# The modulation product of a conditioned encoder layer: from split float32r matmuls to plain float32 on four column groups

## The chip, the cores and the metric

The kernel runs on one core of one Trainium2 chip. The metric is the device time of one execution in microseconds, as a median over runs. Engines are named as the profile names them: PE is TensorE's matmul side, PEld its weight loads, DVE is VectorE, ACT is ScalarE, POOL is GpSimd, SP is SyncE, whose queue issues the loads and stores.

## The reference, cut to what matters

One step of an encoder layer: 512 prompt tokens and 8 sequences of 16 tokens each. Every one of the 9 sequences (1 prompt, 8 samples) has a conditioning vector c of 1024 numbers. Six vectors of 1024 numbers are made of it, two each of shift, scale and gate:

```
m = jax.nn.silu(c) @ w_ada + b_ada            # (9, 1024) @ (1024, 6144)
shift1, scale1, gate1, shift2, scale2, gate2 = split(m, 6)
h = rmsnorm(x) * (1 + scale1) + shift1         # input of the projections and of both attentions
x = x + gate1 * (merge(attentions) @ w_out)
h = rmsnorm(x) * (1 + scale2) + shift2
x = x + gate2 * ((silu(h @ w_gate) * (h @ w_up)) @ w_down)
```

All is float32. The product with w_ada, 24 MB of weights for nine rows, is what the change touches.

## The kernel before, in words

Most products are made of float32r matmuls (one pass over the moving columns). To keep float32's accuracy, each operand is split into a high part (a cast to float32r on ScalarE, L85) and a low part (source minus high, L86, on VectorE or, where `eng=G` is given, on GpSimd), and the products high x high, high x low and low x high are added in PSUM (L92 to L94).

Weights come in granules of 512 KB, 128 partitions by 1024 numbers. `load_raw` (L168) loads one into the pool `w_raw`, which has three buffers for all weights of the kernel; `granule` splits it into `w_hi` and `w_lo`, three buffers each per pool.

`ada_chunk` makes 512 of the 6144 columns of m. Twelve chunks make all. A chunk is four granules of w_ada, each two blocks of 128 rows. The stationary operand is `cT`: per block of 128 rows, 9 columns of the high part of silu(c) and 9 of the low part. For each of the 8 blocks one matmul has the granule's high part as its moving operand (L198) and one its low part (L199), so 16 matmuls of 512 columns add up in 18 rows of one PSUM bank. Row r and row 9 + r belong to sequence r.

These 18 rows are brought together later. `ada_cols` (L211) multiplies blocks of 128 columns of the rows, with the row of b_ada as a nineteenth, by the selector `sel` (19 by 9), and so adds high, low and bias and turns rows into columns. `gate_rows` does the same for the gates with `selr`, which also spreads a sequence's row over its tokens.

Order of the work: the stage of the modulation and the input norm follows a list written out by hand (`steps`): n are key norms of the cached keys of a sequence, x loads and norms of 128 tokens, c loads the selectors, a0 to a3 are the chunks 0 to 3 (shift1 and scale1), h and s modulate. In it three of four granules of a chunk are subtracted on GpSimd (`engs=(None, G, G, G)`), and the chunk's rows stay in SBUF. Chunks 4 to 10 come between the gate blocks that fill the attention of the prompt, chunk 11 at the end of the attention of the sample; their rows go to `ada_d` in DRAM and are loaded again by `ada_rows`. A planner that simulates the engines sets the order in which each engine's instructions stand, so that matmuls of a chunk can stand apart, with others between them.

Other lines that are named: L289 to L298 norm and transpose x, L319 and L320 are squares and sums of the key norms, `lTh` and `lTl` are high and low parts of transposed cached latents, L102 to L109 the reciprocal square root, L395 to L397 products of the rotary tables, L834 and L924 plain float32 matmuls of the attention of the sample: L834 (`absorb`) in batches of four, on partitions 0 to 63 and 64 to 127 in turn, L924 (`mla_values`) five for each of two blocks and eight sequences.

Of the kernel before, what the change touches and what calls it, by code (L numbers as in the profile page):

```python
# [42 lines left out]
QSC = QK ** -0.5  # L43
C_KV, C_QB, C_KB, C_VB, C_G = 384, 672, 1184, 1696, 2208
# [3 lines left out]
def layer_kernel(  # L48
# [47 lines left out]
    def rsqrt(out, ss, inv, pl, n):  # L96
        v = pl.tile([P, n], F32, tag="rs_v", bufs=2, name=nm("rsv"))
        t = pl.tile([P, n], F32, tag="rs_t", bufs=2, name=nm("rst"))
        if not isinstance(inv, list):
            inv = [(0, n, inv)]  # L100
        for a, b, sc in inv:
            V.tensor_scalar(out=v[:, a:b], in0=ss[:, a:b], scalar1=sc, scalar2=EPS, op0=ALU.mult, op1=ALU.add)  # L102
        # a square root of the scalar engine's table, then a Newton step to float32
        for a, b, sc in inv:
            S.activation(out=t[:, a:b], in_=ss[:, a:b], func=AF.Sqrt, scale=sc, bias=eps_t)
        V.reciprocal(out, t)
        V.tensor_tensor(out=t, in0=out, in1=out, op=ALU.mult)  # L107
        V.scalar_tensor_tensor(out=t, in0=t, scalar=-0.5, in1=v, op0=ALU.mult, op1=ALU.mult)
        V.scalar_tensor_tensor(out=out, in0=t, scalar=1.5, in1=out, op0=ALU.add, op1=ALU.mult)  # L109
# [10 lines left out]
    # ---------------------------------------------------------------- constants  # L120
# [10 lines left out]
    # the tensor engine's clock rises while the first loads are under way  # L131
# [8 lines left out]
    sel = ct([19, 9], "sel")  # L140
    selr = ct([19, 2 * P], "selr", F32R)
# [7 lines left out]
    cT = ct([P, KD, 18], "cT", F32R)  # L149

    ada_d = dram.tile([18, 6 * DM], F32, tag="ada_d", name="ada_d")
# [9 lines left out]
    # weight staging: 0.5 MB granules, each split exactly into a high and a low part  # L161
    wa = ctx.enter_context(pool("wstA", side="right"))

    def load_raw(src, shape, rows=P):
        n = shape[0] * shape[1]
        raw = wa.tile([P, 1024], F32, tag="w_raw", bufs=3, name=nm("wraw"))[:rows, :n]
        rv = raw.rearrange("p (k n) -> p k n", k=shape[0])
        nc.sync.dma_start(rv, src)  # L168
        return raw, rv
# [21 lines left out]
    def ada_chunk(pls, rowp, ci, keep=None, engs=(None,)):  # L191
        ps = mm_tile()
        for g in range(4):
            hi, lo = granule(pls[g % len(pls)], w_ada_v[:, 2 * g:2 * g + 2, ci * 512:(ci + 1) * 512], [2, 512],
                             eng=engs[g % len(engs)])
            for j in range(2):
                k = 2 * g + j
                T.matmul(ps[:18, :], cT[:, k, :], hi[:, j, :], start=(k == 0), stop=False)  # L198
                T.matmul(ps[:18, :], cT[:, k, :], lo[:, j, :], start=False, stop=(k == 7))  # L199
        if keep is not None:  # L200
            S.copy(keep, ps[:18, :])
        else:
            row = rowp.tile([18, 512], F32, tag="ada_row", bufs=2, name=nm("adar"))
            S.copy(row, ps[:18, :])
            nc.sync.dma_start(ada_d[:, ci * 512:(ci + 1) * 512], row)
# [14 lines left out]
    # ---------------------------------------------------------------- state of the sample up to its attention  # L220
# [33 lines left out]
    # ---------------------------------------------------------------- modulation, normed input, norms of cached keys  # L254
    with pool("klat") as kp, pool("xin") as xp:
        xnT = xp.tile([P, KD, NT], F32, tag="xnT", name="xnT")
        c_sb = xp.tile([19, DM], F32, tag="rows", bufs=1, name="c_sb")[0:9, :]
# [25 lines left out]
        split(cT[:, :, 0:9], cT[:, :, 9:18], ptv)  # L283
# [41 lines left out]
        def ada_start(ci):  # L325
            if ci % 2 == 0:
                rows[0] = xp.tile([19, DM], F32, tag="rows", bufs=1, name=nm("rows1"))
                nc.sync.dma_start(rows[0][18:19, :], b_ada[:, ci * 512:ci * 512 + DM])
            ada_chunk(AB, None, ci, keep=rows[0][0:18, (ci % 2) * 512:(ci % 2 + 1) * 512], engs=(None, G, G, G))
            if ci == 1:  # L330
                ada_shift(B1, ada_cols(rows[0], 8))
            if ci == 3:
                ada_scale(A1, ada_cols(rows[0], 8), gmix)

        # h^T = xn^T * A + B, split
# [17 lines left out]
        def consts(_):  # L353
            nc.sync.dma_start(sel, sel_tab[:, 2 * P:])
            nc.sync.dma_start(gmix, g_norm_mix[0].rearrange("(k p) -> p k", p=P))
            nc.sync.dma_start(gffn, g_norm_ffn[0].rearrange("(k p) -> p k", p=P))
            V.tensor_copy(selr, load_raw(sel_tab[:, 0:2 * P].unsqueeze(1), [1, 2 * P], 19)[0])
# [5 lines left out]
    # small constants of the attention part  # L363
# [38 lines left out]
    def split3(dst, src, order):  # L402
        # parts of src, 32 columns each, side by side: high and low parts in the order given
        first = order.index("h")
        hi = dst[:, :, first * 32:(first + 1) * 32]
        S.copy(hi, src)
        for i, o in enumerate(order):
            d = dst[:, :, i * 32:(i + 1) * 32]
            if o == "h" and i != first:
                S.copy(d, src)  # L410
            elif o == "l":
                V.tensor_tensor(out=d, in0=src, in1=f(hi), op=ALU.subtract)

    # ---------------------------------------------------------------- projections out of the modulated input
# [216 lines left out]
    # relative-bias table, its clipped far end extended, distance rising along the row  # L631
# [20 lines left out]
    # ---------------------------------------------------------------- attention of the prompt, beside the gates  # L652
# [5 lines left out]
    def gate_block(blk, pl):  # L658
        # sigmoid(z) = (1 + tanh(z / 2)) / 2; the sum and the factor come with the merge
        hi, lo = granule(wa, w_in_v[:, :, C_G + blk * P:C_G + (blk + 1) * P], [KD, P])  # L660
        sg = pl.tile([P, NT], F32, tag="gsg", bufs=2, name=nm("sg"))
        for hf in range(2):
            ps = mm_tile()
            c = slice(hf * HALF, (hf + 1) * HALF)
            for k in range(KD):
                mm3(ps[:, :HALF], hi[:, k, :], lo[:, k, :], hT[:, k, c], hTl[:, k, c], k == 0, k == KD - 1)
                if k % 4 == 3:
                    yield
            S.activation(out=sg[:, c], in_=ps[:, :HALF], func=AF.Tanh, scale=0.5)
        nc.sync.dma_start(gate_d[blk], sg)  # L670
# [3 lines left out]
    def filler(blocks, pl):  # L674
        for n in blocks:
            yield from gate_block(n, pl)
            if n in ADA_AT:
                ada_chunk((wa,), pl, 4 + ADA_AT.index(n))
                yield
# [5 lines left out]
    with pool("pwork") as pw:  # L685
# [17 lines left out]
        def head_in(n):  # L703
            br, h = n // H, n % H
            st = {"br": br, "h": h, "bias": None}
            if h % 2 == 0:
                vn = load_nat(vb_d if br else va_d, P, h // 2 * P, "vnat")
                # stationary of a head: its high and low parts side by side, the high part at the head's rows
                st["v"] = pt_([P, 4, 4, 64], "v", 2, F32R)
                split(st["v"][:, :, 0::3, :], st["v"][:, :, 1:3, :], vn.rearrange("p j (h d) -> p j h d", h=2), eng=G)  # L710
            else:
                st["v"] = heads[n - 1]["v"]
# [86 lines left out]
    # ---------------------------------------------------------------- attention of the sample  # L799
    e2 = {}  # L800
    with pool("ework") as ew:
# [23 lines left out]
        def absorb():  # L825
            # q' = Wk (g qn) per head
# [139 lines left out]
        def band_probs(st):  # L966
            # per pair of heads: stationary [high | low] parts of its 32 rows of probabilities
# [45 lines left out]
        # operations of a step: lower case on the sequence before, upper case on this one  # L1013
# [4 lines left out]
        for s in range(NSEQ + 1):  # L1018
            for op in "N K0 S0 v0 K1 v1 S1 K2 S2 v2 K3 S3 X p v3 K u o Y P A".split():
# [7 lines left out]
                elif s < NSEQ:  # L1027
# [18 lines left out]
                    elif s == NSEQ - 1:  # L1046
                        ada_chunk((wa,), ew, 11)
# [15 lines left out]
    # ---------------------------------------------------------------- merge of the branches  # L1063
# [12 lines left out]
    def ada_rows(c0):  # L1076
        raw = wa.tile([P, 1024], F32, tag="w_raw", bufs=3, name=nm("wraw"))
        nc.sync.dma_start(raw[0:18, :], ada_d[:, c0:c0 + DM])
        nc.sync.dma_start(raw[18:19, :], b_ada[:, c0:c0 + DM])
        return raw[0:19, :]  # L1080

    def gate_rows(c0, scale):
        # rows of a gate, by tokens: of the prompt, of the sample
        raw = ada_rows(c0)
        hi = wa.tile([P, 1024], F32R, tag="w_hi", bufs=3, name=nm("whi"))[0:19, :]
        lo = wa.tile([P, 1024], F32R, tag="w_lo", bufs=3, name=nm("wlo"))[0:19, :]
# [56 lines left out]
    # ---------------------------------------------------------------- output projection, residual, second norm  # L1143
# [79 lines left out]
    # ---------------------------------------------------------------- feed-forward  # L1223
# [61 lines left out]
def _tables():  # L1285
    """Rotary tables of the positions, and selectors of the modulation rows: of the shapes alone."""
# [40 lines left out]
```

## Time and profile before

| | us |
|---|---|
| median of 3 runs | 1216.45 |
| lowest, highest | 1215.79, 1216.54 |
| profiled execution, first to last instruction | 1215.7 |
| TensorE matmuls busy | 1189.0 (98%) |
| VectorE busy | 684.2 (56%) |
| ScalarE busy | 544.3 (45%) |
| GpSimd busy | 137.9 (11%) |

Times in the profile are microseconds from the span's start, durations of single instructions nanoseconds where marked mean ns. A matmul's duration overlaps that of the next; how fast they follow each other is read from start to start. A plain float32 matmul is recorded as two instructions. Shapes stand as partitions x elements; for matmuls rows*columns of the stationary operand, then the moving one.

### The profile page before, as it was taken

Reading aid. Unit: us, or ns where it says so; the run is one execution under the profiler, and the core shown is the slowest. Engines: PE = TensorE matmul, PEld = TensorE weight load, DVE = VectorE, ACT = ScalarE, POOL = GpSimd, SP = SyncE. Lnnn points to the kernel's source line nnn. Section 1 sums busy time; section 2 is a strip of 40 time slices with the busy share of each in tenths; the row PEclk is TensorE's granted clock in tenths of the full one; section 3 lists DMA queues with packets and bytes.
Section 4 is the critical chain, followed back from the end, with each engine's and each line's share of the span. In section 5 each row is a group of like instructions: output and inputs, shape, how many; then the busy total and the mean of one; then the engine's idle time right before and its main releaser. Section 6 shows DMA issues by size and latency. Waiting matters only on the chain. (4 is left out here: it accounts for less than half of the span.)

```text
span 1215.7 us, 19702 instructions
## 1 busy us (share of the span) xinstructions
PE 1189.0 (98%) x7515; PEld 1077.5 (89%) x7515; DVE 684.2 (56%) x1539; ACT 544.3 (45%) x1086; POOL 137.9 (11%) x253
## 2 busy tenths in 40 slices
PE   8889999999999999999999998999999999999998
PEld 6568988999987889899989888999989999889996
DVE  4887566858887775777766437433344233342333
ACT  6775533446776665666653246322112222112210
POOL 2440001010000101334212221000000000000000
PEclk9998999999999999999999998999999999999999
DMA  8651434475655348455367312322123222232111
GB/s 260 227 161 46 127 137 136 159 235 167 184 162 176 119 137 287 138 178 173 95 213 266 103 55 70 88 70 78 62 70 105 70 71 87 67 89 70 70 40 65
DMA packets 159264, 155.30 MB, mean 128 GB/s; under 512 B 24632, under 2 KB 123475, under 8 KB 159170
## 3 DMA queue, kind: packets, MB, share of 16 engines
q1 hardware_dynamic: 159170, 154.05, 40.4%
q8 instruction: 59, 0.97, 0.3%
q14 instruction: 35, 0.29, 0.1%
HBM read 135.15 MB, written 18.88 MB: 127 GB/s over the span
## 5 line engine op out<-in xcount | busy, mean ns | idle before, releaser
L85 ACT CAST whi<-wraw 128x1024 fp32r<-128x1024 f32 (+2 forms) x184 | 190.3, 1038 | 273.4 <-PE mm L94 107.5
L86 DVE TENSOR_TENSOR wlo<-wraw,whi 128x1024 fp32r<-128x1024 f32 (+3 forms) x168 | 203.4, 1213 | 131.6 <-ACT whi L85 127.3
L92 PE MATMUL mm<-h2T,whi 128*128 128x320 f32 x704 | 217.9, 311 | 0.0
L93 PE MATMUL mm<-h2Tl,whi 128*128 128x320 f32 x704 | 217.8, 310 | 0.0
L94 PE MATMUL mm<-h2T,wlo 128*128 128x320 f32 x704 | 217.8, 310 | 0.0
L92 PEld LDWEIGHTS mm<-h2T,whi 128*128 128x128 f32 x704 | 132.9, 189 | 0.4 <-ACT aT L85 0.4
L93 PEld LDWEIGHTS mm<-h2Tl,whi 128*128 128x128 f32 x704 | 132.7, 189 | 0.1
L94 PEld LDWEIGHTS mm<-h2T,wlo 128*128 128x128 f32 x704 | 132.7, 189 | 0.0
L1237 DVE TENSOR_TENSOR sg<-mm,sg 128x320 f32<-128x320 f32 x44 | 21.6, 492 | 121.3 <-PE mm L94 119.3
L93 PE MATMUL mm<-wlo,aT 128*128 128x512 f32 x220 | 85.5, 389 | 0.0
L92 PE MATMUL mm<-whi,aT 128*128 128x512 f32 x220 | 85.5, 389 | 0.0
L94 PE MATMUL mm<-whi,aTl 128*128 128x512 f32 x220 | 85.4, 389 | 0.0
L92 PE MATMUL mm<-hT_hi,whi 128*128 128x320 f32 x256 | 81.5, 318 | 0.0
L94 PE MATMUL mm<-whi,hT_lo 128*128 128x512 f32 (+3 forms) x240 | 79.6, 332 | 0.0
L94 PE MATMUL mm<-hT_hi,wlo 128*128 128x320 f32 x256 | 79.5, 311 | 0.0
L93 PE MATMUL mm<-hT_lo,whi 128*128 128x320 f32 x256 | 79.4, 310 | 0.0
L92 PE MATMUL mm<-whi,hT_hi 128*128 128x512 f32 (+3 forms) x240 | 79.4, 331 | 0.0
L93 PE MATMUL mm<-wlo,hT_hi 128*128 128x512 f32 (+3 forms) x240 | 79.4, 331 | 0.0
L1268 DVE TENSOR_TENSOR tmp<-mm,gate 128x512 f32<-128x512 f32 x30 | 20.7, 690 | 78.7 <-PE mm L94 78.7
L85 ACT CAST aT<-sg 128x320 fp32r<-128x320 f32 x44 | 20.0, 455 | 78.7 <-DVE sg L1237 78.7
L92 PEld LDWEIGHTS mm<-hT_hi,whi 128*128 128x128 f32 x256 | 48.2, 188 | 2.1 <-issue 1.2
L94 PEld LDWEIGHTS mm<-hT_hi,wlo 128*128 128x128 f32 x256 | 48.1, 188 | 1.2 <-DVE wlo L86 0.3
(343 smaller groups left out, 2672.4 us busy)
## 6 DMA issues: line engine op xcount, KB each, us to landing
wraw<-in_w_ada_dram SPq DMA_DIRECT2D x48, 512.0 KB
wraw<-in_w_in_dram SPq DMA_DIRECT2D x28, 512.0 KB
wraw<-in_w_gate_dram SPq DMA_DIRECT2D x22, 512.0 KB
wraw<-in_w_up_dram SPq DMA_DIRECT2D x22, 512.0 KB
wraw<-in_w_down_dram SPq DMA_DIRECT2D x22, 512.0 KB
lat<-in_cache_kv_latent_dram SPq DMA_DIRECT2D x16, 512.0 KB
wraw<-in_cache_band_v_dram SPq DMA_DIRECT2D x16, 512.0 KB
kn<-in_cache_band_k_dram SPq DMA_DIRECT2D x16, 512.0 KB
```

The lines of the kernel that those rows point to most:

```text
L85: S.copy(hi, src)
L86: (eng or V).tensor_tensor(out=lo, in0=src, in1=f(hi), op=ALU.subtract)
L92: T.matmul(out, lh, rh, start=start, stop=False)
L93: T.matmul(out, lh, rl, start=False, stop=False)
L94: T.matmul(out, ll, rh, start=False, stop=stop)
L1237: V.tensor_tensor(out=sg, in0=pu[:, :HALF], in1=sg, op=ALU.mult)
L1268: V.tensor_tensor(out=tmp, in0=ps, in1=gate2[t // 4][:, cc], op=ALU.mult)
```

## The change

The product is made in plain float32, so nothing of w_ada and of silu(c) is split any more. A matmul has 32 columns of the stationary operand (9 of silu(c), the rest zeros) and writes one of four groups of 32 PSUM partitions: block k of the 8 goes to group k mod 4, and a group adds up two blocks. The four groups of a chunk are added later by the same selectors, which now have 106 rows (9 in each group of 32, and the bias).

```
+AR = 3 * 32 + 9 + 1
...
-    sel = ct([19, 9], "sel")
-    selr = ct([19, 2 * P], "selr", F32R)
+    sel = ct([AR, 9], "sel")
+    selr = ct([AR, 2 * P], "selr", F32R)
+    G.memset(sel, 0.0)
...
-    cT = ct([P, KD, 18], "cT", F32R)
-    ada_d = dram.tile([18, 6 * DM], F32, tag="ada_d", name="ada_d")
+    cT = ct([P, KD, 32], "cT")
+    V.memset(cT, 0.0)
+    ada_d = dram.tile([AR - 1, 6 * DM], F32, tag="ada_d", name="ada_d")
...
-    def load_raw(src, shape, rows=P):
+    def load_raw(src, shape, rows=P, given=P):
...
-        nc.sync.dma_start(rv, src)
+        if given < rows:
+            G.memset(raw, 0.0)
+        nc.sync.dma_start(rv[:given], src)
...
-    def ada_chunk(pls, rowp, ci, keep=None, engs=(None,)):
+    def ada_chunk(rowp, ci, keep=None):
         ps = mm_tile()
         for g in range(4):
-            hi, lo = granule(pls[g % len(pls)], w_ada_v[:, 2 * g:2 * g + 2, ci * 512:(ci + 1) * 512], [2, 512],
-                             eng=engs[g % len(engs)])
+            rv = load_raw(w_ada_v[:, 2 * g:2 * g + 2, ci * 512:(ci + 1) * 512], [2, 512])[1]
             for j in range(2):
                 k = 2 * g + j
-                T.matmul(ps[:18, :], cT[:, k, :], hi[:, j, :], start=(k == 0), stop=False)
-                T.matmul(ps[:18, :], cT[:, k, :], lo[:, j, :], start=False, stop=(k == 7))
+                q = slice(32 * (k % 4), 32 * (k % 4) + 32)
+                T.matmul(ps[q, :], cT[:, k, :], rv[:, j, :], start=(k < 4), stop=(k >= 4))
         if keep is not None:
-            S.copy(keep, ps[:18, :])
+            S.copy(keep, ps[:AR - 1, :])
         else:
-            row = rowp.tile([18, 512], F32, tag="ada_row", bufs=2, name=nm("adar"))
-            S.copy(row, ps[:18, :])
+            row = rowp.tile([AR - 1, 512], F32, tag="ada_row", bufs=2, name=nm("adar"))
+            S.copy(row, ps[:AR - 1, :])
             nc.sync.dma_start(ada_d[:, ci * 512:(ci + 1) * 512], row)
...
-        split(cT[:, :, 0:9], cT[:, :, 9:18], ptv)
+        S.copy(cT[:, :, 0:9], ptv)
...
         def consts(_):
-            nc.sync.dma_start(sel, sel_tab[:, 2 * P:])
+            raw = load_raw(sel_tab[0:9, 0:2 * P].unsqueeze(1), [1, 2 * P], AR, 9)[0]
+            nc.sync.dma_start(sel[AR - 1:AR, :], sel_tab[18:19, 2 * P:])
+            nc.sync.dma_start(raw[AR - 1:AR, :], sel_tab[18:19, 0:2 * P])
+            for q in range(4):
+                nc.sync.dma_start(sel[32 * q:32 * q + 9, :], sel_tab[0:9, 2 * P:])
+                if q:
+                    nc.sync.dma_start(raw[32 * q:32 * q + 9, :], sel_tab[0:9, 0:2 * P])
...
-            V.tensor_copy(selr, load_raw(sel_tab[:, 0:2 * P].unsqueeze(1), [1, 2 * P], 19)[0])
+            V.tensor_copy(selr, raw)
```

Everywhere else 18 rows become 105 and 19 become 106: the tiles `rows`, the rows that `ada_rows` loads, and their split in `gate_rows`.

## Rows read from the trace of the kernel before

**Rows 1.** Page: busy us (share of the span) and instructions of each engine.

```profile
PE 1189.0 (98%) x7515; PEld 1077.5 (89%) x7515; DVE 684.2 (56%) x1539; ACT 544.3 (45%) x1086; POOL 137.9 (11%) x253
```

**Rows 2.** Windows: stretch, length, busy (count) of PE PEld DVE ACT POOL, clock, DMA.

```profile
25.00:45.00 20.00, 15.90 (x71) 10.05 (x70) 17.66 (x40) 13.45 (x24) 8.07 (x4) 0.91 0.74 252
...
270.00:465.00 195.00, 195.00 (x1230) 166.00 (x1229) 157.02 (x426) 135.04 (x303) 8.68 (x12) 1.00 0.53 161
465.00:620.00 155.00, 149.47 (x1360) 142.18 (x1358) 105.52 (x265) 97.62 (x221) 48.19 (x178) 1.00 0.53 169
```

**Rows 3.** Groups by line, TensorE, by shape: count, busy us, mean ns, idle before.

```profile
L198 PE MATMUL mm<-whi,cT 128*18 128x512 f32 x96 | 39.7, 413 | 0.0
...
L924 PE MATMUL mm<-PT,lat 128*128 128x128 f32 x128 | 18.1, 275 | 0.0
...
L211 PE MATMUL tr<-sel,rows 19*128 19x9 f32 x32 | 4.2, 255 | 1.1 <-ACT rows L201 1.1
```

**Rows 4.** Timeline of TensorE inside chunk 9: start us, us, instruction.

```profile
426.11 0.39 PE L198 MATMUL mm<-whi,cT 128*18 128x512 f32 x1
...
427.27 0.40 PE L199 MATMUL mm<-wlo,cT 128*18 128x512 f32 x1
```

**Rows 5.** Timeline of TensorE, 488 to 493 us, neighbours of one kind merged.

```profile
488.13 0.31 PE L94 MATMUL mm<-hT_hi,wlo 128*128 128x320 f32 x1
488.38 2.26 PE L834 MATMUL mm<-qnT,wkT 64*128 64x128 f32 x24
...
491.59 1.16 PE L834 MATMUL mm<-qnT,wkT 64*128 64x128 f32 x8
```

**Rows 6.** Line L834: duration ns least/median/most, first and last start.

```profile
L834 PE MATMUL mm<-qnT,wkT x32: 272/272/373, 488.4 to 492.5; 64*128 64x128 f32 x32
```

**Rows 7.** Groups by line and shape, ScalarE, VectorE, GpSimd (GpSimd before 90 us).

```profile
L85 ACT CAST whi<-wraw 128x1024 fp32r<-128x1024 f32 x174 | 182.3, 1051 | 268.8 <-PE mm L94 107.5 <-PE mm L93 99.4 <-DMA wraw<-in_w_up_dram 16.0
...
L86 DVE TENSOR_TENSOR wlo<-wraw,whi 128x1024 fp32r<-128x1024 f32 x158 | 192.9, 1223 | 128.7 <-ACT whi L85 124.3 <-DMA kn<-in_cache_band_k_dram 1.4 <-PE mm L94 1.1
...
L86 POOL TENSOR_TENSOR wlo<-wraw,whi 128x1024 fp32r<-128x1024 f32 x12 | 29.1, 2432 | 42.0 <-ACT whi L85 26.6 <-DVE rn_all L109 9.5 <-PE mm L199 5.8
```

**Rows 8.** Timeline of VectorE.

```profile
29.74 0.23 DVE L396 TENSOR_TENSOR rq_s<-rq_s,gqr_bc 128x80 f32<-128x80 f32 x1
29.89 2.38 DVE L397 TENSOR_TENSOR rq_s<-rq_s,gqr_bc 128x80 f32<-128x80 f32 x1
...
47.23 2.07 DVE L107 TENSOR_TENSOR rst<-rn_all 128x32 f32<-128x32 f32 x1
```

**Rows 9.** Timeline of GpSimd.

```profile
29.77 2.40 POOL L86 TENSOR_TENSOR wlo<-wraw,whi 128x1024 fp32r<-128x1024 f32 x1 [0.74 <-ACT whi L85]
41.73 7.53 POOL L86 TENSOR_TENSOR wlo<-wraw,whi 128x1024 fp32r<-128x1024 f32 x3 [9.55 <-DVE rn_all L109]
```

**Rows 10.** Timeline of TensorE in the first stage; in brackets idle time and releaser.

```profile
28.14 0.40 PE L93 MATMUL mm<-wk_lo,lTh 128*128 128x512 f32 x1
29.87 0.50 PE L94 MATMUL mm<-wk_hi,lTl 128*128 128x512 f32 x1 [1.33 <-DVE lTl L86]
...
30.45 0.40 PE L93 MATMUL mm<-wk_lo,lTh 128*128 128x512 f32 x1
33.61 0.79 PE L94 MATMUL mm<-wk_hi,lTl 128*128 128x512 f32 x1 [2.77 <-DVE lTl L86]
...
49.26 0.40 PE L198 MATMUL mm<-whi,cT 128*18 128x512 f32 x1
50.41 0.96 PE L94 MATMUL mm<-wk_hi,lTl 128*128 128x512 f32 x3 [0.75 <-DVE rsv L102]
```

**Rows 11.** Window, TensorE alone: stretch, length, busy (count), granted clock, DMA, GB/s.

```profile
33.70:37.00 3.30, 3.30 (x8) 0.50 0.99 350
```

**Rows 12.** Timeline of SP's queue: start us, us of issuing.

```profile
6.31 0.29 SPq L354 DMA_DIRECT2D sel<-in_sel_tab_dram  x1
...
11.25 0.37 SPq L168 DMA_DIRECT2D wraw<-in_w_ada_dram  x1
```

More of the change, by code (lines that the diff above doesn't have):

```diff
@@ L256, in layer_kernel @@
         xnT = xp.tile([P, KD, NT], F32, tag="xnT", name="xnT")
-        c_sb = xp.tile([19, DM], F32, tag="rows", bufs=1, name="c_sb")[0:9, :]
+        c_sb = xp.tile([AR, DM], F32, tag="rows", bufs=1, name="c_sb")[0:9, :]
         nc.sync.dma_start(c_sb[0:1, :], c_prompt)
@@ L326, in ada_start @@
             if ci % 2 == 0:
-                rows[0] = xp.tile([19, DM], F32, tag="rows", bufs=1, name=nm("rows1"))
-                nc.sync.dma_start(rows[0][18:19, :], b_ada[:, ci * 512:ci * 512 + DM])
-            ada_chunk(AB, None, ci, keep=rows[0][0:18, (ci % 2) * 512:(ci % 2 + 1) * 512], engs=(None, G, G, G))
+                rows[0] = xp.tile([AR, DM], F32, tag="rows", bufs=1, name=nm("rows1"))
+                nc.sync.dma_start(rows[0][AR - 1:AR, :], b_ada[:, ci * 512:ci * 512 + DM])
+            ada_chunk(None, ci, keep=rows[0][0:AR - 1, (ci % 2) * 512:(ci % 2 + 1) * 512])
             if ci == 1:
@@ L677, in filler @@
             if n in ADA_AT:
-                ada_chunk((wa,), pl, 4 + ADA_AT.index(n))
+                ada_chunk(pl, 4 + ADA_AT.index(n))
                 yield
@@ L1046, in layer_kernel @@
                     elif s == NSEQ - 1:
-                        ada_chunk((wa,), ew, 11)
+                        ada_chunk(ew, 11)
             mla, band = mla_n, nxt
@@ L1077, in ada_rows @@
         raw = wa.tile([P, 1024], F32, tag="w_raw", bufs=3, name=nm("wraw"))
-        nc.sync.dma_start(raw[0:18, :], ada_d[:, c0:c0 + DM])
-        nc.sync.dma_start(raw[18:19, :], b_ada[:, c0:c0 + DM])
-        return raw[0:19, :]
+        nc.sync.dma_start(raw[0:AR - 1, :], ada_d[:, c0:c0 + DM])
+        nc.sync.dma_start(raw[AR - 1:AR, :], b_ada[:, c0:c0 + DM])
+        return raw[0:AR, :]
     def gate_rows(c0, scale):
         raw = ada_rows(c0)
-        hi = wa.tile([P, 1024], F32R, tag="w_hi", bufs=3, name=nm("whi"))[0:19, :]
-        lo = wa.tile([P, 1024], F32R, tag="w_lo", bufs=3, name=nm("wlo"))[0:19, :]
+        hi = wa.tile([P, 1024], F32R, tag="w_hi", bufs=3, name=nm("whi"))[0:AR, :]
+        lo = wa.tile([P, 1024], F32R, tag="w_lo", bufs=3, name=nm("wlo"))[0:AR, :]
         split(hi, lo, raw)
```

## The prediction, made before the changed kernel was run

> **What bounds the kernel now.** I read the page first: TensorE is busy for 98% of the span [rows 1]. An average can hide a stage with another limit, so next come the windows by stage. From 270 to 465 us TensorE has no gap at all, from 25 to 45 us it is busy for 15.9 us of 20, and from 465 to 620 us for 149.5 of 155 [rows 2]. The reader is to see two regimes. In the middle, only TensorE's own instructions count, and time freed on ScalarE or VectorE is worth nothing. In the first 62 us TensorE also waits, so there the splitting work can matter. The four chunks 0 to 3 of the modulation product lie in the first 80 us; chunks 4 to 10 lie in the attention of the prompt and chunk 11 at 605 us, where TensorE is the bound.
>
> Third come the groups by line. L198 and its twin L199 run 96 times each [rows 3]. Their mean of 413 ns overlaps the next instruction; what counts is the distance from start to start, read in the timeline: six starts from 426.11 to 427.27 us, (427.27 - 426.11) / 5 = 0.232 us [rows 4]. A chunk of 16 thus costs 16 x 0.232 = 3.71 us, and a granule (a load of two blocks of 128 rows, four matmuls) 0.93 us.
>
> **What is removed.** 192 matmuls at 0.232 us = 44.5 us of TensorE; 48 casts on ScalarE at 1.05 us; 36 subtractions on VectorE at 1.22 us and 12 on GpSimd at 2.43 us [rows 7].
>
> **What is added on TensorE: 96 plain float32 matmuls of 32 columns by 512.** The trace has no such matmul, but it has plain float32 ones of another shape. Each is recorded as two instructions: L924 is called 64 times with lat (8 sequences, 2 blocks, 4 keys) and shows x128 [rows 3]. So 96 calls become 192 instructions, as many as before, and the question is what one costs and how many run at once.
>
> Cost of one, called U. The last eight of L834 (128 columns) take 1.16 us for x8 [rows 5]; less the last one's 0.272 and the 0.373 - 0.272 = 0.10 by which the first waits for its weights [rows 6], 0.79 / 7 = 0.112 us from start to start. Four times as many columns give at most 4 x 0.112 = 0.448 us. L211, with only 9 columns, lasts nearly as long (255 against 275 ns [rows 3]), so part of 0.112 may be the weight load, and 0.448 is an upper bound. From below, a plain pass is not quicker than the 0.232 of the same columns in one pass. I take 0.448, since L834 and L924 are of the same kind and L198 is not. The Trainium skill (FP8 and Floating Point Precision, TensorE Precision Notes) says that true float32 takes four passes through the array; as an estimate that is 4 x 512 / 2.4 GHz = 0.853 us a matmul, 0.427 an instruction, and the sum below would end some 2 us lower; no row here separates the passes.
>
> How many at once. Every matmul of before starts at the first column, so no row shows column groups side by side. The nearest are the row groups of L834: three batches of eight, on rows 0 to 63 and 64 to 127 in turn. One after another, 24 would have 0.10 + 23 x 0.112 = 2.68 us from first start to last; measured is 2.26 - 0.27 = 1.99 [rows 5]. The 0.69 saved are six instructions at two borders, three at each: one batch's tail runs beside the next one's head, and more than the two neighbours overlap. I take it that column groups behave likewise: four streams at once. This is the step with most doubt.
>
> Length of a run. Raw granules live in a pool of three. Before, the split freed a slot; now a slot is held until TensorE has read it, so at most three of a chunk's four granules are at hand together. In the middle I reckon with a run of six matmuls and one of two per chunk (8 chunks), in the first stage with runs of two, as the granules come one by one (16 runs). Each run costs 0.1 us to enter: L834 starts 0.25 us after the L94 ahead of it, whose 320 columns need 0.13 at 2.4 GHz [rows 5]; bounds 0 and 0.2. With four streams, a run of two takes 2 U + 0.1 = 1.00 us against 0.93, and a run of six, in which two groups serve twice, 4 U + 0.1 = 1.89. First stage: 16 x 0.07 = **+1.1 us**. Middle: 8 x (1.89 + 1.00 - 3.71) = **-6.6 us**.
>
> **What the splits gave back.** While GpSimd subtracts (29.77 us, for 2.40) VectorE's L397 takes 2.38 us, where its neighbour L396, of the same kind, takes 0.23; at 47.23 a small L107 takes 2.07 under three GpSimd subtractions that begin at 41.73 [rows 8, 9]. TensorE waits behind these: 29.87 - 28.14 - 0.23 = 1.50 us, 33.61 - 30.45 - 0.23 = 2.93 us (both for lTl), 50.41 - 49.26 - 0.23 = 0.92 us [rows 10]. After the second wait the granted clock is 0.50 (1.2 GHz) for 3.3 us [rows 11], which costs half of that, 1.7 us. With no GpSimd subtraction there, all four can go: 1.50 + 2.93 + 0.92 + 1.7 = **-7.0 us**; at worst nothing, if TensorE is then late for the next load instead. ScalarE's and VectorE's other savings are costed at nothing: behind 195.0 busy us of 195 nobody waits for them [rows 2]; without that cover the 36 VectorE subtractions alone would be worth 44 us.
>
> **What is moved or grows.** The selectors now come in ten loads in place of two, all in SP's queue ahead of the first w_ada granule. From the load of sel to that granule's issue SP takes 11.25 - 6.31 = 4.9 us for five issues; one plain issue is 0.29 [rows 12]. Eight more are 2.4 to 3 us by which x, cached keys and w_ada come later; TensorE has work of loads already made, so I take **+1.0 us**, bounds 0 and 3. Behind the cast of selr, which waits for those loads, stand VectorE's norms; the same bound covers it. The memset of cT and sel, and results of 105 rows in place of 18 (copies by columns, a write of 215 KB per chunk), are costed at nothing: their cover is the same full TensorE; without it they are a microsecond in all.
>
> Sum: +1.1 - 6.6 - 7.0 + 1.0 = -11.5 us, from a span of 1215.7 to 1204.2. The median of the runs, 1216.45, is 0.75 above the span, so the forecast is **1205 us**.
>
> **The rivals.** *Two streams only.* If a record may not start before the one ahead of it has, then a group's second record waits for its first, and the next group stands behind both: just the second of one and the first of the next run together, and n matmuls take n + 1 units. A run of two costs 3 U + 0.1 = 1.44 us, a run of six 7 U + 0.1 = 3.24. That is 16 x 0.51 = +8.2 and 8 x (3.24 + 1.44 - 3.71) = +7.8; with -7.0 and +1.0, +10 us: 1226. For it: the two records of a matmul stand side by side. Against it: three overlaps at a border of L834, where this allows one. The Trainium skill (TensorE: Matmul & The Clock Gate, Part 3, The mechanism) states this order, matmuls starting and ending strictly in program order. The trace agrees only in part, since the 1.99 us of L834 need more than one overlap per border, unless the batches were interleaved in the queue.
>
> *No streams at once (the change does not do what its groups are for).* All instructions run singly: a run of two 4 U + 0.1 = 1.89, a chunk 16 U + 0.2 = 7.37. 16 x 0.96 + 8 x 3.66 = +44.7, with -6.0 +38.7: 1255 us. This is the case on the slower side; it decides as soon as U exceeds 0.23 by more than the 6 us pay for, at U = 0.25. For it: no row shows two column groups, and each would need its own stream of all 128 rows. Against it: L834's two groups do run together.
>
> *Cheap passes.* With U = 0.232 and four streams a chunk's runs cost 6 x 0.232 + 0.2 = 1.59 us and the sum is some -30 us, 1187. Against it: two records of 128 columns never start less than 0.11 apart within a group.
>
> **How the numbers follow.** Four streams 0.47, with its own range 1192 to 1217 (units of 0.40, whole chunks in one run, against no stall recovered, 3 us of queue and entries of 0.2); two streams 0.22; none 0.28; cheap passes 0.03. The range 1192 to 1254 leaves out the cheap passes, the fastest tenth of the first case and the upper half of the third. About 0.2%, 2.4 us, is what a measurement of this kernel can tell from no change. Faster: 0.44 of the first case and the last, 0.47. Same: the upper end of the first and the lower of the second, 0.07. Slower: 0.46.
>
> **What would show it.** In the changed profile: 192 records of 512 columns with 32 active columns; four of them starting within some ns of one another and the next four 0.45 us later (four streams), or pairs (two), or single starts 0.45 apart (none). No GpSimd work on w_ada, no VectorE instruction of 128x32 over 1 us before 62 us, TensorE's waits for lTl near 30 us gone and the granted clock there at 1.0. The prediction is wrong if column groups do not overlap, if TensorE waits on w_ada loads because slots are freed late, or if the first stage's stalls only move.

## The result, and the profile after

The changed kernel takes 1246.82 us (median of 4 runs, 1244.86 to 1248.15) where the kernel before took 1216.12 beside it (4 runs, 1214.93 to 1216.54): a ratio of 1.0255, 95% interval 1.0241 to 1.027. It is 30.7 us slower; the forecast was 1205. The profiled execution has a span of 1244.8 us.

First the page of the changed kernel (busy us, share, instructions) against [rows 1]:

```profile
PE 1197.8 (96%) x7515; PEld 1075.8 (86%) x7515; DVE 637.4 (51%) x1503; ACT 502.4 (40%) x1038; POOL 102.5 (8%) x243
```

TensorE has as many instructions as before, but its share fell from 98% to 96%: it waits more, while every other engine has less to do. The windows, with the columns of [rows 2], say where:

```profile
25.00:45.00 20.00, 15.28 (x76) 8.69 (x76) 11.24 (x40) 9.58 (x22) 0.00 (x0) 0.91 0.72 233
45.00:62.00 17.00, 17.00 (x89) 10.37 (x85) 9.62 (x24) 8.72 (x18) 0.00 (x0) 1.00 0.76 248
...
270.00:465.00 195.00, 181.06 (x1109) 150.32 (x1108) 122.47 (x369) 101.61 (x251) 8.59 (x12) 0.95 0.51 150
465.00:620.00 155.00, 147.08 (x1278) 137.84 (x1277) 98.74 (x252) 91.03 (x205) 43.80 (x176) 0.98 0.54 169
```

From 45 to 62 us TensorE has no gap. But from 270 to 465 us, where TensorE had 195.00 busy us of 195 at a clock of 1.00, it now has 181.06 at 0.95. This is the stretch that the change was to shorten.

How much each stage gained is read from the timelines: the start of a stage's first instruction, before and after. First projection, first gate block, first L834 (L846 after), first instruction of the output projection; before:

```profile
101.04 0.30 PE L92 MATMUL mm<-whi,hT_hi 128*128 128x288 f32 x1
...
255.75 0.31 PE L92 MATMUL mm<-hT_hi,whi 128*128 128x320 f32 x1
...
488.38 0.37 PE L834 MATMUL mm<-qnT,wkT 64*128 64x128 f32 x1
...
684.17 0.39 PE L92 MATMUL mm<-whi,mT 128*128 128x512 f32 x1
```

and after:

```profile
93.10 0.40 PE L93 MATMUL mm<-whi,hT_hi 128*128 128x288 f32 x1 [2.27 <-ACT jk L325]
...
249.48 0.31 PE L93 MATMUL mm<-hT_hi,whi 128*128 128x320 f32 x1
...
508.29 0.37 PE L846 MATMUL mm<-qnT,wkT 64*128 64x128 f32 x1
...
713.68 0.40 PE L93 MATMUL mm<-whi,mT 128*128 128x512 f32 x1
```

The differences of such starts, for these two kernels and for five of the experiments below (us):

| stage | before | after | split slots | fourth elsewhere | two raw | one group | no GpSimd |
|---|---|---|---|---|---|---|---|
| to the first projection | 101.0 | 93.1 | 91.8 | 98.4 | 88.5 | 100.6 | 93.4 |
| to the first gate block | 154.7 | 156.4 | 155.8 | 154.2 | 154.3 | 158.9 | 154.7 |
| attention of the prompt, chunks 4 to 10 | 232.6 | 258.8 | 224.3 | 245.8 | 222.8 | 260.8 | 232.7 |
| to the output projection, with chunk 11 | 195.8 | 205.4 | 202.1 | 206.0 | 204.8 | 208.2 | 198.0 |
| to the end | 531.5 | 531.1 | 529.7 | 531.2 | 531.1 | 530.2 | 530.7 |

After against before: -7.9, +1.7, +26.2, +9.6 and -0.4 us. The first stage gained what it was to gain; the loss lies with chunks 4 to 10.

**The matmuls themselves went as forecast.** The timeline of TensorE in the first run of chunk 0 (start, length, instruction; a merged row lasts from its first start to its last end), from three windows of it:

```profile
25.54 0.64 PE L205 MATMUL mm<-wraw,cT 128*32 128x512 f32 x4
...
26.00 1.03 PE L205 MATMUL mm<-wraw,cT 128*32 128x512 f32 x6
...
26.43 1.03 PE L205 MATMUL mm<-wraw,cT 128*32 128x512 f32 x4
...
25.54 1.91 PE L205 MATMUL mm<-wraw,cT 128*32 128x512 f32 x12
```

The first row holds four records and lasts 0.64 us, and one record 0.59: the four start within 0.05 us, one in each column group (with a single group, in the experiment of one group a granule below, the records start one after another). The next four begin at 26.00; the second row also holds the pair of 26.43, and the third that pair and the one of 26.85. So four streams at once, and a unit of 0.43 to 0.46 us, against U = 0.448. The estimate from the Trainium skill (FP8 and Floating Point Precision, TensorE Precision Notes) of 0.427 an instruction agrees with the later steps of 0.43.

**What went wrong is what stands around a run.** The queue of SP (start, time of issuing, load) in the attention of the prompt:

```profile
269.44 0.37 SPq L174 DMA_DIRECT2D wraw<-in_w_ada_dram  x1
269.91 1.05 SPq L174 DMA_DIRECT2D wraw<-in_w_in_dram  x2
...
274.72 0.49 SPq L174 DMA_DIRECT2D wraw<-in_w_ada_dram  x1
...
277.73 2.25 SPq L174 DMA_DIRECT2D wraw<-in_w_ada_dram  x2
...
303.63 0.37 SPq L174 DMA_DIRECT2D wraw<-in_w_ada_dram  x1
304.10 1.17 SPq L174 DMA_DIRECT2D wraw<-in_w_in_dram  x2
```

and TensorE beside it (in brackets idle time and releaser):

```profile
268.35 1.91 PE L205 MATMUL mm<-wraw,cT 128*32 128x512 f32 x12
...
273.62 1.05 PE L205 MATMUL mm<-wraw,cT 128*32 128x512 f32 x4 [0.37 <-DMA wraw<-in_w_ada_dram]
276.50 0.41 PE L93 MATMUL mm<-hT_hi,whi 128*128 128x320 f32 x1 [1.82 <-ACT whi L86]
...
302.54 1.91 PE L205 MATMUL mm<-wraw,cT 128*32 128x512 f32 x12
308.82 1.63 PE L205 MATMUL mm<-wraw,cT 128*32 128x512 f32 x4 [2.27 <-DMA wraw<-in_w_ada_dram]
```

Read the two together. Three loads for a chunk are issued from 274.72 to 279.98 and fill the raw pool of three. They stay there until the run of six reads them at 302.54, 22.6 us after the last of them was issued. Only then, at 303.63 and 304.10, does SP issue the chunk's fourth granule and the two w_in granules of the next gate block. SP's own waits from 250 to 480 us name the matmuls of the chunks as what released a load (total, times, longest):

```profile
SPq L174 <- PE mm L205: 18.7, 21, 2.7
```

TensorE runs out of work it may do: 2.27 us for w_ada here, and 1.82 us for the split of w_in one chunk earlier. All waits of TensorE from 250 to 480 us (total, times, longest):

```profile
PE mm L205 <- DMA wraw<-in_w_ada_dram: 7.7, 7, 2.3
PE mm L93 <- ACT whi L86: 5.5, 4, 1.8
PE tr L139 <- DVE Pr L662: 4.2, 3, 2.2
```

That is 17.4 us (the last line, 4.2 us, waits for results of the softmax, not for a load), and around the waits the granted clock falls:

```profile
250.00:480.00 230.00, 212.47 (x1305) 175.11 (x1304) 136.12 (x403) 118.00 (x287) 11.32 (x16) 0.95 0.53 154
```

The falls are to the lower level, 1.2 GHz: 0.50 right behind the wait of 2.27 us, for instance (window, busy TensorE, clock):

```profile
309.20:312.60 3.40, 3.40 (x13) 0.50 1.24 262
```

A mean of 0.95 over 230 us is worth 0.05 x 230 = 11.5 us. With 17.5 us idle that makes 29; less the 5.7 us that seven chunks were to save, 23 of the 26.2 us of the stage; where the last 3 us lie stays open.

The queue and the waits have two readings. Either the fourth load comes late, and what it holds up is late with it (**late fourth load**); or the slots are the matter: while three w_ada granules stand in the raw pool, no w_in granule can be loaded (**held slots**). The Trainium skill (Perfetto Trace Analysis, Optimization Strategy) says that a gap which repeats on the engine that should be saturated can mean that there is no room for the next tile; the rows here fit, but don't say which tile.

### The profile page after: what moved, and what is told of

Same layout as the page of the kernel before. It is cut to its first block, busy times and chain, and to the rows that moved or that the text cites. A ratio compares the mean times of both kernels' runs of the same rounds, so it can differ in the third digit from the quotient of the medians.

```text
span 1244.8 us, 19516 instructions
## 1 busy us (share of the span) xinstructions
PE 1197.8 (96%) x7515; PEld 1075.8 (86%) x7515; DVE 637.4 (51%) x1503; ACT 502.4 (40%) x1038; POOL 102.5 (8%) x243
## 5 line engine op out<-in xcount | busy, mean ns | idle before, releaser
L86 ACT CAST whi<-wraw 128x1024 fp32r<-128x1024 f32 (+2 forms) x136 | 140.1, 1034 | 253.1 <-PE mm L95 108.9
L87 DVE TENSOR_TENSOR wlo<-wraw,whi 128x1024 fp32r<-128x1024 f32 (+3 forms) x132 | 158.2, 1202 | 142.8 <-ACT whi L86 139.4
L93 PE MATMUL mm<-hT_hi,whi 128*128 128x320 f32 x256 | 84.1, 329 | 5.5 <-ACT whi L86 5.5
L205 PE MATMUL mm<-wraw,cT 128*32 128x512 f32 x192 | 41.5, 640 | 12.9 <-DMA wraw<-in_w_ada_dram 12.9
```

Of the source, the lines that this page charges most:

```text
L87: (eng or V).tensor_tensor(out=lo, in0=src, in1=f(hi), op=ALU.subtract)
L93: T.matmul(out, lh, rh, start=start, stop=False)
L205: T.matmul(ps[q, :], cT[:, k, :], rv[:, j, :], start=(k < 4), stop=(k >= 4))
```

## The experiments

**Split slots.** The w_ada granules go, unsplit, into the buffers of the high and low parts, which are three each; the raw pool is left to w_in.

```
-            rv = load_raw(w_ada_v[...], [2, 512])[1]
+            tg = ("w_hi", "w_lo")[g % 2]
+            rv = f(wa.tile([P, 1024], F32R, tag=tg, bufs=3, ...))
+            nc.sync.dma_start(rv, w_ada_v[...])
```

> As the changed kernel, but a w_ada granule is loaded into the buffers that held the high and low parts (w_hi and w_lo, three of each, in turn), so all four granules of a chunk can be on hand and the three raw buffers stay free for the other weights. Slots theory (the 29 us come from loads that are issued late because a raw buffer is held until TensorE has read it): the waits for w_ada and for the next block's high part in the middle go, the attention of the prompt no longer loses 26 us but gains 5 to 14, and the time is 1200 to 1212 us. Rival, the price of the column-group runs themselves (entering, leaving, the planner's order of neighbours): the time stays at 1235 or more. Rival, transfer time (the loads are slow whenever they are issued): half of the loss stays, 1220 to 1235.

1205.88 us, ratio 0.990 (0.9882 to 0.9919): 41 us less than the changed kernel, with the same matmuls. In the attention of the prompt a chunk is one run now (the last one in two pieces); the row of one in the timeline, the instruction behind it, and the window:

```profile
265.52 1.92 PE L207 MATMUL mm<-wada,cT 128*32 128x512 f32 x16
267.38 0.33 PE L93 MATMUL mm<-kTh,qTh 96*128 96x128 f32 x1
...
250.00:480.00 230.00, 226.72 (x1543) 198.64 (x1541) 148.79 (x439) 130.55 (x325) 20.79 (x53) 1.00 0.65 190
```

Eight matmuls take 267.38 - 265.52 = 1.86 us (forecast for a whole chunk: 4 U + 0.1 = 1.89), the clock is 1.00 again. The buffers were the cause of the loss.

**One load a chunk.** Only the first granule of a chunk is loaded and all eight matmuls read it; three quarters of w_ada are left out.

> As the changed kernel, but only the first of a chunk's four granules is loaded and all eight matmuls of the chunk read it (three quarters of w_ada are left out): 12 loads in place of 48, the same matmuls. Slots theory: no run waits for a late fourth load, so the middle is as good as the matmuls allow, 4 units of 0.45 us for a chunk in one run; together with the first stage the time is 1190 to 1207 us. If the runs themselves cost the time, it stays at 1235 or more.

1194.97 us, ratio 0.9808 (0.9788 to 0.9829). Its attention of the prompt takes 222.8 us against 224.3 with split slots: once the slots are right, loading the other three quarters costs that stage 1.5 us. Most of the 11 us between the two lies later, on the way to the output projection: 196.0 us against 202.1.

**One group a granule.** Both blocks of a granule in the same column group, so that a run of two has one group to itself.

```
-                q = slice(32 * (k % 4), 32 * (k % 4) + 32)
-                T.matmul(ps[q, :], ..., start=(k < 4), stop=(k >= 4))
+                q = slice(32 * g, 32 * g + 32)
+                T.matmul(ps[q, :], ..., start=(j == 0), stop=(j == 1))
```

> As the changed kernel, but both blocks of a granule go to the same column group (group g for granule g), so that a run of two matmuls has one stream and a run of six has three. If a group's records may start ahead of an earlier group's (one queue for each group), a run of six still takes four units of 0.45 us, 1.8 us, with three starts together; if matmuls start strictly in program order it takes about 10 units, 4.5 us. A run of two takes four units in place of two: over the 24 such runs up to 21 us more work for TensorE, of which what lies beside a wait for loads is hidden; time 1250 to 1270 us. If column groups shared nothing of the gain, the time would be that of the changed kernel.

1260.68 us, ratio 1.0351 (1.0324 to 1.0378). A run of six (three groups) and a run of two (one group), from the timeline:

```profile
278.33 0.64 PE L205 MATMUL mm<-wraw,cT 128*32 128x512 f32 x3
...
278.33 1.93 PE L205 MATMUL mm<-wraw,cT 128*32 128x512 f32 x12
...
284.13 0.62 PE L205 MATMUL mm<-wraw,cT 128*32 128x512 f32 x1 [0.87 <-DMA wraw<-in_w_ada_dram]
...
284.13 1.90 PE L205 MATMUL mm<-wraw,cT 128*32 128x512 f32 x4 [0.87 <-DMA wraw<-in_w_ada_dram]
```

With one group the records start singly and four of them last as long as twelve over three groups. The groups do pay. The program writes the four records of group 0 of a run of six ahead of the others, yet three groups start together; the trace gives starts and not the order of the queue, which the planner sets, so that an instruction looks past others of the queue is argued and not shown. In the first stage, where eight runs of two and one of four each last 1.90 - 1.05 = 0.85 us longer than after the change, the first projection comes 100.6 - 93.1 = 7.5 us later (9 x 0.85 = 7.7).

**Before without GpSimd.** The kernel before, with all splits of w_ada on VectorE.

```
-            ada_chunk(AB, None, ci, keep=..., engs=(None, G, G, G))
+            ada_chunk(AB, None, ci, keep=..., engs=(None,))
```

> The kernel before with one edit: the 12 subtractions of the first stage that ran on GpSimd run on VectorE. Theory that GpSimd holds VectorE up there: VectorE's instructions of 2 us on 128x32 become 0.2, the half-clock stretch at 34 us goes, and the first projection starts 3 to 8 us earlier than 101 us, so 1208 to 1213 us. Rival, the first stage's gain of the change came from fewer casts on ScalarE and fewer subtractions in all: the 12 moved subtractions (15 us of VectorE) take the place of the stalls and the time is the same or longer, 1215 to 1222 us.

1208.89 us, ratio 0.993 (0.9913 to 0.9948). Two groups of VectorE, against [rows 8], and the window of the first stage (TensorE's busy time first, its clock 1.00):

```profile
L397 DVE TENSOR_TENSOR rq_s<-rq_s,gqr_bc 128x80 f32<-128x80 f32 x1 | 0.2, 234 | 0.0
L396 DVE TENSOR_TENSOR rq_s<-rq_s,gqr_bc 128x80 f32<-128x80 f32 x1 | 0.2, 233 | 0.0
...
0.00:93.44 93.44, 84.17 (x432) 63.01 (x432) 71.81 (x155) 71.72 (x126) 5.67 (x10) 1.00 0.69 211
```

L397 takes 0.23 us in place of 2.38, no L107 on 128x32 takes over 0.19 (2.07 before), and the first projection comes 7.6 us earlier, though VectorE has twelve subtractions more. The stalls were GpSimd's, and taking them away needs no column groups. Two things went together here, VectorE's instructions that GpSimd stretched and subtractions that take 2.43 us on GpSimd against 1.22 on VectorE [rows 7]; no run separates them.

**Fourth elsewhere.** As changed, but the fourth granule of a chunk in a buffer of the high parts: it is never late.

```
+            if g == 3:
+                rv = f(wa.tile([P, 1024], F32R, tag="w_hi", bufs=3, ...))
+                nc.sync.dma_start(rv, src)
+            else:
                 rv = load_raw(src, [2, 512])[1]
```

> The fourth granule of a chunk goes into a buffer of the high parts; the first three stay in the raw pool of three. If the loss comes from the fourth load, which has to wait for a slot and holds the queue (late fourth load), a chunk becomes one run of eight again, TensorE's waits for w_ada and for the next block's high part go, the granted clock from 250 to 480 us is 1.00, and the time is that of the split slots, 1206 to 1209 us. If the loss comes from the three raw slots being held until TensorE has read them (held slots), the next block's w_in still comes late: 8 waits of about 2 us and most of the clock drops stay, and the time is 1225 to 1240.

1236.51 us, ratio 1.0153 (1.0132 to 1.0175): a quarter of the 41 us comes back (1246.8 to 1236.5 is 10 us), the rest does not. By stage it is 13 us in the attention of the prompt (258.8 to 245.8), while the first stage takes 5.3 us more (98.4 against 93.1, with a wait of 5.22 us for w_ada at 42.73). TensorE's largest wait from 250 to 480 us, then SP and TensorE at one chunk:

```profile
PE mm L93 <- ACT whi L86: 12.4, 7, 2.4
```

```profile
306.23 1.00 SPq L174 DMA_DIRECT2D wraw<-in_w_in_dram  x2
...
305.14 1.48 PE L210 MATMUL mm<-wraw,cT 128*32 128x512 f32 x10
...
311.97 0.41 PE L93 MATMUL mm<-hT_hi,whi 128*128 128x320 f32 x1 [1.47 <-ACT whi L86]
```

The wait for w_ada is gone, and that for the split of w_in rose from 5.5 to 12.4 us. The chunk starts at 305.14, the two w_in loads are issued at 306.23, when its first blocks are read, and the gate block begins at 311.97. Held slots, then, with the late fourth load on top of it.

**Fourth on GpSimd's queue.** As changed, but GpSimd issues the fourth load, so that the w_in loads don't stand behind it.

> As the changed kernel, but the fourth granule's load is issued by GpSimd and not by SP, still into the raw pool; the two w_in loads behind it no longer stand in its queue. If the wait for w_ada itself costs the time (late fourth load), the run of two still comes late and the time stays within a few us of 1246. If it is the queue behind it (w_in late, then split and matmul late), the waits for the high part go and the time falls to 1215 to 1230. In both cases TensorE's waits for w_ada stay.

1253.04 us, ratio 1.029 (1.0258 to 1.0322). TensorE's waits for w_in's split and for w_ada from 250 to 480 us:

```profile
PE mm L93 <- ACT whi L86: 13.1, 6, 4.1
PE mm L211 <- DMA wraw<-in_w_ada_dram: 1.9, 1, 1.9
```

Nothing is gained: the wait for the split of w_in rose from 5.5 to 13.1 us. That the waits for w_ada stay, as was expected in both cases, was wrong. They fell from 7.7 to 1.9 us, and five of the seven runs of two now stand behind the start of the next gate block. At one chunk the run of six starts at 310.87, the two w_in loads are issued from 312.02 on, the fourth granule by GpSimd at 312.23. That the loads stand behind one another in SP's queue is not what costs; both need the slots that the run of six frees.

**Two raw, one raw.** The same as split slots, for g >= 2 and for g >= 1 alone: a chunk holds two raw slots, or one.

> Only the first two granules of a chunk in the raw pool, the last two in a buffer of the high and one of the low parts; all four fit at once. Held slots: one slot stays free for the first w_in load of the next block, the second load still waits until TensorE has read a pair; the time lies between the fourth granule elsewhere (1236) and the split slots (1206), about 1220 to 1228. Late fourth load: no load waits for TensorE, 1206 to 1209, no other than the next run.

> Only the first granule in the raw pool. Held slots: two slots are free, as many as the two w_in loads of the next block need, so the waits for the high part go and the time is that of the split slots, 1205 to 1212. If the loss grows evenly with each slot held, it is a third of the way from 1206 to 1236, 1216.

1204.31 us (ratio 0.9895, 0.9871 to 0.9918) and 1207.21 (0.9916, 0.9893 to 0.9939): both as good as split slots. The number expected for two raw, 1220 to 1228, was wrong: the cost doesn't grow evenly with the slots held, it comes with the third. SP and TensorE of two raw show why:

```profile
278.13 0.37 SPq L174 DMA_DIRECT2D wraw<-in_w_in_dram  x1
...
292.65 0.43 SPq L174 DMA_DIRECT2D wraw<-in_w_in_dram  x1
...
290.62 1.06 PE L211 MATMUL mm<-wraw,cT 128*32 128x512 f32 x8
291.50 1.04 PE L211 MATMUL mm<-wada,cT 128*32 128x512 f32 x8
...
293.64 0.39 PE L93 MATMUL mm<-hT_hi,whi 128*128 128x320 f32 x1
```

Through the free slot the next block's first w_in granule is loaded at 278.13, 12.5 us ahead of the chunk, and its block begins at 293.64 without a wait. From three slots held to two (1236.5 to 1204.3 us) 32 us come back, 23 of them in the attention of the prompt (245.8 to 222.8) and 10 in the first stage (98.4 to 88.5).

**Middle only.** Split slots in chunks 4 to 11; the first stage loads into the raw pool.

> The split slots in chunks 4 to 11 only; chunks 0 to 3 of the first stage load into the raw pool, as in the changed kernel. If the held slots cost nothing in the first stage, as its marks in the changed kernel show (first projection at 93.1 us against 91.8 with the split slots), 1206 to 1208; if a part of the 41 us between the two kernels comes from the first stage, 1210 or more.

1205.14 us, ratio 0.9898 (0.9877 to 0.9919), the time of the split slots. The first stage has no part in the loss.

**Two selector loads.** Split slots, and the selectors from a table of 106 rows.

> The split slots, and the selectors from a table of 106 rows in two loads in place of ten, without the two memsets of GpSimd. The prediction's term: 1.0 us less than the split slots (1204.9 against 1205.9, ratio to before 0.989), bounds 0 and 3. Rival: TensorE had enough to do and the loads cost nothing, 1205.9.

1205.4 us (1200.97 to 1210.72), ratio 0.9909 (0.9885 to 0.9934) beside 0.990: eight issues less can't be told from nothing within that spread.

## Why the prediction was wrong

**Wrong: "Length of a run".** Its mechanism held: "a slot is held until TensorE has read it", a run of six and one of two per chunk. But a price was put only on the matmuls of the two runs and on entering them, and the wait for what the held slots keep out was costed at nothing. The term "Middle: 8 x (1.89 + 1.00 - 3.71) = -6.6 us" stands against +26.2 us over chunks 4 to 10. Two things are missing. The fourth load waits for the run of six, which costs that stage 13 us (258.8 to 245.8, fourth elsewhere against changed). And the raw pool also serves the w_in granules, which as long as w_ada fills it are not loaded; with a slot free for them another 23 us come back there (245.8 to 222.8, two raw against fourth elsewhere). Before, ScalarE's cast and a subtraction emptied a slot soon after it was filled; with the splits removed, emptying depends on TensorE, the engine that is furthest behind. The removed splits were work, but also what freed the pool. The prediction's last sentence names "TensorE waits on w_ada loads because slots are freed late", but no rival had it with a price. The clock belongs to that price: the half-speed stretches after the waits cost about as many us as two thirds of the waits (11.5 beside 17.5). That the time measured lies below the upper bound of 1254 is luck: the range reached so far up for the rival without streams, which the trace refutes.

**Right: four streams and U.** Four records start within 0.05 us of one another, the unit is 0.43 to 0.46 us against 0.448, and a whole chunk in one run takes 1.86 against 1.89. Both rivals on this point fall. *Two streams* rested on the order that the Trainium skill states (TensorE: Matmul & The Clock Gate, Part 3, The mechanism); the trace does not agree, as long as the two records of a matmul stand side by side in the queue, since the second record of an earlier group starts about 0.45 us after the first one of a later group. The trace doesn't hold the order of the queue, but one run of chunk 10 speaks for it: both records of a single matmul come ahead of L782.

```profile
468.69 1.05 PE L205 MATMUL mm<-wraw,cT 128*32 128x512 f32 x2
469.67 0.50 PE L782 MATMUL mm<-PTl,v 128*128 128x512 f32 x1
```

*No streams* falls too: 1255 lies near the time measured, but by another cause. *Cheap passes* falls with U.

**Right in sum, in part by luck: the first stage.** Forecast +1.1 - 7.0 + 1.0 = -4.9, measured -7.9. That GpSimd's subtractions cost this stage is shown by the kernel before without them, -7.6 at the first projection. But the term of -7.0 named four places, and they did not simply go. The waits for lTl near 30 us are gone, yet a wait of 2.94 us for w_ada comes at 38.32, the granted clock behind it (39.5 to 42.9 us) is 0.50 again, and from 25 to 45 us it is 0.91, as before. Here the stalls "only move", as the prediction's last sentence has it. The stage as a whole, before and after, with the columns of [rows 2]:

```profile
0.00:101.04 101.04, 88.58 (x433) 65.66 (x433) 76.70 (x148) 72.71 (x127) 35.35 (x22) 0.95 0.63 195
...
0.00:93.10 93.10, 83.48 (x432) 58.90 (x433) 51.68 (x131) 53.09 (x102) 6.05 (x12) 0.98 0.63 198
```

TensorE's idle time went from 12.5 to 9.6 us, -2.9, and what the clock takes from 0.05 x 101 to 0.02 x 93 us, about -3. A part of the latter is a stretch of the kernel before that the prediction didn't name: 0.50 from 91.7 to 98.5 us, behind a wait of 2.31 us for lTh. The runs were fewer than the 16 counted on: eight of two, one of four, two of six, by the forecast's prices 8 x 1.00 + 1.00 + 2 x 1.89 = 12.8 us in place of 4 x 3.71 = 14.8, that is -2.0 for +1.1. The three make -8 for the -7.9 measured. The selectors' +1.0 is within its bounds and not resolved.

**What the column groups are worth.** Split slots save some 8 us (232.6 to 224.3) in the attention of the prompt against before (the forecast's price for seven whole chunks is 7 x 1.82 = 12.7), and lose 4.1 us against the kernel before without GpSimd on the way to the output projection. The net is 1208.89 against 1205.88 us: the intervals of the two ratios overlap (0.9913 to 0.9948, 0.9882 to 0.9919), but every run of the first (1208.58 to 1211.25) is slower than every run of the second (1205.39 to 1206.29). Of the 12 us that split slots gain on the kernel before (1218.07 us beside both), taking GpSimd out gains 9 without any column groups. The 4.1 us lie near the waits for t (2.2 and 1.2 us of TensorE in that stage), one of 1.4 for b_ada and more time at the lower clock (0.97 against 0.98 over the stage). The results of 105 rows don't cost them by themselves: one load a chunk writes the same rows, takes 196.0 us for that stage, as before the change (195.8), and waits 0.2 us for t. Whether it is the order of the loads or the planner's order of the rest, no run separated, and it stays open. The versions with split slots, one or two raw, and those in the middle only are the fastest that load all of w_ada, 1204 to 1207 us, and differ by about as much as the planner's order alone may change: the way to the output projection takes 202.1 us with split slots and 199.5 with them in the middle only, for the same program text.

## What to carry to other kernels

When a step that copies data out of a staging buffer is removed, ask who frees the buffer now, how long it is held, and what else is loaded through the same pool: here one slot of three left free was worth 23 us in the stage that had lost 26. A lower count of instructions and less busy engines say nothing of it; read the queue of loads beside the engine that has become the one to free the slots. Test a gain that has two sources one by one: the cheap one (GpSimd off VectorE's way) brought 9 of 12 us.

## What was not expected of the hardware

Plain float32 matmuls of different column groups run side by side whichever group the program writes first: 12 records that it writes in the order of group 0, 0, 0, 0, 1, ... began as three at once and took 1.93 us, where four in a single group took 1.90. TensorE then starts instructions ahead of earlier ones of its queue, if the queue holds the two records of a matmul side by side, as the run of chunk 10 suggests. And a subtraction of 2.4 us on GpSimd stretches a VectorE instruction of 0.23 us with two inputs in SBUF to 2.38; the Trainium skill (GPSIMD Engine Reference, 1. Specifications) names this contention, and the kernel before without GpSimd shows it gone at 0.23 us.
